# Transposed queries with high and low rows exchanged: by two DMAs instead of by a swapped copy and a second transpose

## The chip, the cores and the metric

The kernel runs on one core of a Trainium2 chip. The metric is the device time of one execution in microseconds (us), the median of several runs. The engines are TensorE (PE in the rows; PEld is its weight load), VectorE (DVE), ScalarE (ACT), GpSimd (POOL) and SyncE (SP, which issues DMAs). A "q" behind an engine's name is its queue of instructions. L619 is line 619 of the kernel.

## The reference, cut to what matters

One layer over a sequence of 1024 frames of width 1024: a mixer of two attention branches, then a SwiGLU feed-forward. The change touches how the queries of both branches reach the score matmuls.

```python
h = rms_norm(x, ln_mix_pre)
z = h @ w_in                      # differential q, k, v | latents | rotary key | gates
q1, q2, k1, k2 = rope(...)        # 8 heads, two 64-wide halves each
o1 = chunk_causal_attention(q1, k1, va, da_scale)
o2 = chunk_causal_attention(q2, k2, va, da_scale)
oa = rms_norm(o1 - lam * o2, da_subln) * (1 - lambda_init)
...
qb_full = concat([qb_nope, rope(qb_rope)])     # 8 heads, 128 + 64 wide
kb_full = concat([kb_nope, rope(k_rope)])      # the rotary key is shared by the heads
ob = chunk_causal_attention(qb_full, kb_full, vb, MLA_QK_DIM ** -0.5)
merged = sigmoid(g_a) * (oa @ w_proj_a) + sigmoid(g_b) * (ob @ w_proj_b)
x = x + rms_norm(merged @ w_o, ln_mix_post)
x = x + rms_norm(swiglu(rms_norm(x, ln_ffn_pre)), ln_ffn_post)
```

All of it is float32. Attention is causal in chunks of 64 frames.

## The kernel before

**High and low parts.** Every float32 operand of a matmul is split into a high part in TensorE's rounded format (float32r) and a low part, the difference. A product is three matmuls: high by high, high by low, low by high (`mm3`, lines 267 to 269). Where the inner dimension is only 64 wide, the kernel puts the high part into rows 0 to 63 and the low part into rows 64 to 127 of one 128-row operand. Keys are held that way: `kT` has the high rows above the low rows. A score tile then takes two matmuls that add up in PSUM (`v` = 0 and 1): one with the query in the same order (high by high plus low by low), one with the query in the exchanged order (low above high). So each query tile is needed transposed in both orders.

**The query tiles before.** A query tile has 128 frames on the partitions, and for each half `m` 64 high columns followed by 64 low columns. `swapped` (lines 615 to 621) has GpSimd copy it with the two column blocks exchanged, two instructions (lines 619 and 620). `pre(i)` then transposes the tile and the swapped copy on TensorE: in differential attention (DA) four transposes into one PSUM bank (lines 689 and 690, twice each, for two halves), in latent attention (MLA) two (lines 904 and 905). ScalarE copies the bank to SBUF, 512 columns (line 693) or 256 (line 908). The result is `Q_[i]`, from which `front(i)` takes `lhsT` by `m` and `v` (lines 707 and 925).

**Stages.** Normalisation, transposed input and the first head's projection come first (to about 66 us). DA runs over eight heads, each over eight query tiles from the last to the first. Beside each head stand fillers: gate tiles, latent projections and the next head's projections. MLA runs over eight heads in the same way, with the next head's projections as fillers; beside its last head stands the first branch projection. After it come the branch and output projections and the feed-forward.

**Order of the work.** The source emits per step x of a head (`pipeline`):

```python
if x + PRE < NT:
    pre(order[x + PRE])      # PRE = 1
if x < NT:
    front(order[x])          # scores, maximum, exponential
...
    back(order[x - depth])   # normalise, transpose the probabilities; depth 1 (DA), 2 (MLA)
```

`tail` (the product with the values) follows every second `back`. This is the order of priority; the order in which each engine gets its instructions is made when the program is built, by a scheduler with its own estimate of durations, and it moves fillers between them. Each engine then works in its own order and waits on semaphores.

**Buffers.** SBUF and PSUM are managed by hand: a zone gives out the block that has been free longest. `z_c` (2048 columns) holds the transposed queries, the swapped copies and a few small tiles; `ps_a` are two PSUM banks that all transposes and the value products share. All DMAs are issued on SP's queue.

Of the kernel before, what the change touches and what calls it, by code (L numbers as in the profile page):

```python
# [12 lines left out]
F32R = mybir.dt.float32r  # L13
# [5 lines left out]
P = 128  # L19
# [150 lines left out]
def kernel(  # L170
# [27 lines left out]
    nc = tc.nc  # L198
# [31 lines left out]
    idr = big.tile([P, P], F32R, name="idr")  # L230
# [9 lines left out]
    def st(tag, n=1):  # L240
        return small.tile([P, n], F32, tag=tag, name=tag)
# [8 lines left out]
    def f32v(ap):  # L250
        return ap.bitcast(F32)
# [48 lines left out]
    z_c, z_ct = Zone(mr, (32768, 34816)), Zone(mr, (34816, AR_COLS))  # L300
# [11 lines left out]
    ps_s, ps_p, ps_a = Banks(mp, 0, 4), Banks(mp, 4, 6), Banks(mp, 6, 8)  # L312
# [299 lines left out]
                       c4[:, 0:nk, 0, half], c4[:, 0:nk, 1, half])  # L612
            tb.free()

    def swapped(q, m):

        b = z_c.alloc(m * P)
        b3 = b.v("p (m c) -> p m c", m=m)
        nc.gpsimd.tensor_copy(b3[:, :, 0:64], f32v(q[:, :, 64:128]))  # L619
        nc.gpsimd.tensor_copy(b3[:, :, 64:128], f32v(q[:, :, 0:64]))  # L620
        return b

    def new_ct(j):
        n = 2 * j + 2
        ct = [z_ct.alloc(512 * min(4, n - g)) for g in range(0, n, 4)]
        last = ct[-1].v("p (k h s) -> p k h s", h=2, s=256)
        nc.gpsimd.memset(f32v(last[:, (n - 1) % 4, :, 0:P]), 0.0)  # L627
        return ct

    def pv(o, ct, vget, j):  # L630
        n = 2 * j + 2
        for kb in range(n):
            c4 = ct[kb // 4].v("p (k h s) -> p k h s", h=2, s=256)
            vh, vl = vget(kb)
            mm3(o, vh, vl, c4[:, kb % 4, 0, :], c4[:, kb % 4, 1, :], kb == 0, kb == n - 1)
# [44 lines left out]
    def da_attn(n, slots, neg_lam, sub8):  # L680
        Q_, P_, CT = {}, {}, {}

        def pre(i):
            q = slots[i // 2]["q"][:, i & 1]
            qx = swapped(q, 2)
            tb = ps_a.alloc()
            for m in range(2):
                a, b = tb.ap[:, m * 256:m * 256 + P], tb.ap[:, m * 256 + P:m * 256 + 256]
                nc.tensor.transpose(a.bitcast(F32R), q[:, m, :], idr)
                nc.tensor.transpose(b.bitcast(F32R), qx.ap[:, m * P:(m + 1) * P], idr)  # L690
            qx.free()
            Q_[i] = z_c.alloc(512)
            nc.scalar.copy(Q_[i].ap, tb.ap)
            tb.free()

        def front(i):
            j = i // 2
            W = P * (i + 1)
            nb = 2 if W > 512 else 1
            qs = Q_.pop(i)  # L700
            nm, ss = st("nm", 2), st("sm", 2)
            pp = []
            for m in range(2):
                sb = ps_s.alloc(nb)
                for p in range(j + 1):
                    for v in range(2):
                        nc.tensor.matmul(sb.ap[:, p * 256:(p + 1) * 256], lhsT=qs.ap[:, m * 256 + v * P:m * 256 + v * P + P],  # L707
                                         rhs=slots[p]["kT"][:, m, :], start=(v == 0), stop=(v == 1))
                pb = f_gen.alloc(W)
                softmax_part(sb.ap, i, m, nm, ss, pb.ap)  # L710
                sb.free()
                pp.append(pb)
            qs.free()
            P_[i] = (pp, ss)

        def back(i):
            pp, ss = P_.pop(i)
            j = i // 2
            if i & 1:
                CT[j] = new_ct(j)  # L720
            rs = st("rs", 2)
            nc.vector.reciprocal(rs, ss)
            bb = st("bb")
            nc.vector.tensor_tensor(out=bb, in0=rs[:, 1:2], in1=neg_lam, op=ALU.mult)
            nc.vector.tensor_scalar_mul(pp[1].ap, pp[1].ap, bb)
            nc.vector.scalar_tensor_tensor(out=pp[0].ap, in0=pp[0].ap, scalar=rs[:, 0:1], in1=pp[1].ap, op0=ALU.mult, op1=ALU.add)
            pp[1].free()
            transposed_probs(pp[0].ap, i, CT[j])
            pp[0].free()

        def tail(j):
            ct = CT.pop(j)
            pb = ps_a.alloc()
            o = pb.ap[:, 0:256]
            pv(o, ct, lambda kb: (slots[kb // 2]["V"][:, kb % 2, 0, :], slots[kb // 2]["V"][:, kb % 2, 1, :]), j)
            for b in ct:
                b.free()
            slots[j]["blk"].free()
            o2, os = f_gen.alloc(256), f_gen.alloc(256)
            nc.scalar.activation(out=o2.ap, in_=o, func=ACTF.Square)  # L740
            nc.scalar.mul(os.ap, o, sub8)  # L741
            pb.free()
            nc.sync.dma_start(s_oa[n * P:(n + 1) * P, j * 256:(j + 1) * 256], os.ap)
            os.free()
            sq = z_c.alloc(512)
            split_sbuf(o2.ap, sq.ap[:, 0:256], sq.ap[:, 256:512], "dve")
            o2.free()

            def sums():
                rb = ps_a.alloc()  # L750
                for h in range(2):
                    nc.tensor.matmul(rb.ap[0:1, 0:256], lhsT=ones_r[:, 0:1], rhs=sq.ap[:, h * 256:(h + 1) * 256],
                                     start=(h == 0), stop=(h == 1))
                sq.free()
                row = f_gen.alloc(256)
                nc.scalar.copy(row.ap[0:1], rb.ap[0:1, 0:256])
                rb.free()
                nc.sync.dma_start(s_ms[n:n + 1, j * 256:(j + 1) * 256], row.ap[0:1])
                row.free()

            return [sums]

        return pipeline(pre, front, back, tail, DA_DEPTH)


# [130 lines left out]
    def mla_attn(M, n, H):  # L896
        vv = H["v"].v("p (t h n d) -> p t h n d", t=NT, h=2, n=2)
        Q_, P_, CT = {}, {}, {}

        def pre(i):  # L900
            q = H["qr"][:, i, :]
            qx = swapped(q.unsqueeze(1), 1)
            tb = ps_a.alloc()
            nc.tensor.transpose(tb.ap[:, 0:P].bitcast(F32R), q, idr)
            nc.tensor.transpose(tb.ap[:, P:2 * P].bitcast(F32R), qx.ap, idr)
            qx.free()
            Q_[i] = z_c.alloc(256)
            nc.scalar.copy(Q_[i].ap, tb.ap[:, 0:256])
            tb.free()

        def front(i):
            j = i // 2
            W = P * (i + 1)
            nb = 2 if W > 512 else 1
            qs = Q_.pop(i)
            nm, ss = st("nm", 2), st("sm", 2)
            sb = ps_s.alloc(nb)
            sl = slice(i * P, (i + 1) * P)
            step = max(W // nb, 256)
            for c in range(nb):  # L920
                ks = slice(c * step, (c + 1) * step)
                o = sb.ap[:, c * 512:c * 512 + step]
                mm3(o, H["q"][:, 0, sl], H["q"][:, 1, sl], H["k"][:, 0, ks], H["k"][:, 1, ks], True, False)
                for v in range(2):
                    nc.tensor.matmul(o, lhsT=qs.ap[:, v * P:(v + 1) * P], rhs=M.kr.ap[:, ks], start=False, stop=(v == 1))
            qs.free()
            pb = f_gen.alloc(W)
            softmax_part(sb.ap, i, 0, nm, ss, pb.ap, W // nb)
            sb.free()
            P_[i] = (pb, ss)  # L930

        def back(i):
            pb, ss = P_.pop(i)
            j = i // 2
            if i & 1:
                CT[j] = new_ct(j)
            rs = st("rs", 2)
            nc.vector.reciprocal(rs[:, 0:1], ss[:, 0:1])
            nc.vector.tensor_scalar_mul(pb.ap, pb.ap, rs[:, 0:1])
            transposed_probs(pb.ap, i, CT[j])  # L940
            pb.free()

        def tail(j):
            ct = CT.pop(j)
            pb = ps_a.alloc()
            o = pb.ap[:, 0:256]
            pv(o, ct, lambda kb: (vv[:, kb, 0, n % 2, :], vv[:, kb, 1, n % 2, :]), j)
            for b in ct:
                b.free()
            os = f_gen.alloc(256)  # L950
            nc.scalar.copy(os.ap, o)
            pb.free()
            nc.sync.dma_start(s_ob[n * P:(n + 1) * P, j * 256:(j + 1) * 256], os.ap)
            os.free()
            if j == 0:
                for b in H["blks"]:
                    b.free()
                if n == NH - 1:
                    M.kr.free()
            return []  # L960

        return pipeline(pre, front, back, tail, MLA_DEPTH)


# [473 lines left out]
```

## Time and profile before

| | |
|---|---|
| median of 3 runs | 2032.49 us (2032.35 to 2034.26) |
| profiled execution | 2036.9 us, span 2035.0 us |
| TensorE busy | 1976.3 us, 97% of the span |
| VectorE, ScalarE, GpSimd busy | 1156.2, 864.2, 541.0 us |
| mean granted clock of TensorE | 0.992 |

The span runs from the first to the last instruction of the profiled execution, which has its own time beside the runs' median. Busy time is the union of an engine's instructions; matmuls are pipelined, and their durations overlap. Issuing a DMA and waiting on a semaphore don't count as busy.

### The profile page before, as it was taken

The page shows a single profiled execution, that of the slowest core. Times are in us where ns is not written, and L with a number is a line of the kernel's source. Part 1 is how long each engine was busy: PE and PEld are TensorE (multiplying, and loading weights), DVE is VectorE, ACT ScalarE, POOL GpSimd, SP SyncE. Part 2 cuts the span into 40 slices and gives each one's busy share as a digit, 9 for nine tenths or more (in the row PEclk, how much of TensorE's full clock was granted, in tenths as well). Part 3 has the DMA queues.
Part 4 walks back from the last instruction along what each step waited for, and adds up shares of the span by engine and source line. Part 5 has one row for each costly group of instructions (what it writes and reads, how often), then busy time and mean ns, then how long its engine had stood idle before and what let it go on. Part 6 is the DMA issues. An engine that isn't in the chain of part 4 may idle for free. (4 is left out here: it accounts for less than half of the span.)

```text
span 2035.0 us, 29108 instructions
## 1 busy us (share of the span) xinstructions
PE 1976.3 (97%) x10656; PEld 1715.3 (84%) x10656; DVE 1156.2 (57%) x2464; ACT 864.2 (42%) x1912; POOL 541.0 (27%) x652
## 2 busy tenths in 40 slices
PE   6999999999999999999999998979999999999998
PEld 6898999999898988988978786757888888888886
DVE  7756757676675667786752354575344444353335
ACT  5445444554544446666653333343333333341102
POOL 2000010200000012222121222356564564462214
PEclk9999999999999999999999999989999999999999
DMA  5212111211212031450043533223222222272204
GB/s 169 69 47 81 44 55 53 57 49 42 77 29 80 29 116 50 130 177 29 32 136 103 176 125 103 85 71 94 73 94 84 71 95 73 95 237 83 83 32 145
DMA packets 148494, 176.52 MB, mean 87 GB/s; under 512 B 13536, under 2 KB 117376, under 8 KB 148352
## 3 DMA queue, kind: packets, MB, share of 16 engines
q1 hardware_dynamic: 148352, 174.68, 27.3%
q8 instruction: 83, 1.36, 0.3%
q14 instruction: 59, 0.48, 0.1%
HBM read 130.54 MB, written 44.11 MB: 86 GB/s over the span
## 5 line engine op out<-in xcount | busy, mean ns | idle before, releaser
L267 PE MATMUL PS<-AR 128*128 128x512 f32 (+3 forms) x2216 | 795.1, 361 | 4.0 <-ACT AR L254 2.5
L269 PE MATMUL PS<-AR 128*128 128x512 f32 (+3 forms) x2216 | 786.3, 356 | 2.6 <-POOL AR L256 2.6
L268 PE MATMUL PS<-AR 128*128 128x512 f32 (+3 forms) x2216 | 784.5, 355 | 3.7 <-POOL AR L256 3.7
L254 ACT CAST AR<-AFm 128x512 fp32r<-128x512 f32 (+4 forms) x514 | 301.7, 610 | 514.1 <-PE PS L1216 207.4
L267 PEld LDWEIGHTS PS<-AR 128*128 128x128 f32 x2216 | 418.1, 189 | 56.8 <-ACT AR L260 3.5
L268 PEld LDWEIGHTS PS<-AR 128*128 128x128 f32 x2216 | 419.0, 189 | 47.8 <-POOL AR L256 4.5
L269 PEld LDWEIGHTS PS<-AR 128*128 128x128 f32 x2216 | 417.9, 189 | 46.3 <-POOL AR L256 3.5
L256 POOL TENSOR_TENSOR AR<-AFm,AR 128x512 fp32r<-128x512 f32 (+4 forms) x203 | 309.2, 1529 | 461.7 <-ACT AR L254 397.4
L1216 PE MATMUL PS<-AR 128*128 128x512 f32 x1848 | 425.7, 392 | 6.1 <-POOL AR L256 4.9
L1216 PEld LDWEIGHTS PS<-AR 128*128 128x128 f32 x1848 | 349.3, 189 | 82.2 <-POOL AR L256 6.2
L256 DVE TENSOR_TENSOR AR<-AFm,AR 128x512 fp32r<-128x512 f32 (+5 forms) x311 | 213.1, 714 | 109.3 <-ACT AR L254 81.8
L260 ACT CAST AR<-PS 128x512 fp32r<-128x512 f32 (+3 forms) x320 | 134.5, 440 | 149.5 <-DVE AFm L388 75.4
L1225 DVE TENSOR_TENSOR AFm<-AFm,PS 128x512 f32<-128x512 f32 x110 | 75.2, 684 | 180.3 <-PE PS L1216 179.6
L261 DVE TENSOR_TENSOR AR<-PS,AR 128x512 fp32r<-128x512 f32 (+3 forms) x320 | 152.9, 496 | 38.0 <-ACT AR L260 36.5
L619 POOL CAST AR<-AR 128x128 fp32r<-128x128 f32 (+1 forms) x128 | 43.1, 337 | 456.0 <-PE PS L690 262.4
L649 ACT ACTIVATE AFm<-PS,nm 128x1024 f32<-128x1024 f32 (+3 forms) x192 | 142.5, 745 | 45.9 <-DVE nm L648 28.8
L648 DVE TENSOR_REDUCE nm<-PS 128x1 f32<-128x1024 f32 (+3 forms) x192 | 143.5, 751 | 3.2
L1288 DVE TENSOR_TENSOR AFm<-AFm,PS 128x512 f32<-128x512 f32 x80 | 54.4, 685 | 103.1 <-PE PS L269 103.1
L1180 DVE TENSOR_TENSOR AFm<-AFm 128x512 f32<-128x512 f32 x66 | 70.4, 1066 | 68.4 <-DMA s_aa<-AFm 29.7
L627 POOL MEMSET AR<- 128x256 f32 x64 | 22.3, 349 | 295.3 <-PE PS L269 200.3
L707 PE MATMUL PS<-AR 128*128 128x256 f32 x640 | 94.9, 290 | 0.1
L609 PE MATMUL PS<-idf,AFm 128*128 128x128 f32 x576 | 88.6, 275 | 2.2 <-ACT AFm L741 0.9
(133 smaller groups left out, 1551.9 us busy)
## 6 DMA issues: line engine op xcount, KB each, us to landing
AFm<-in_w_in_dram SPq DMA_DIRECT2D x72, 192.0 KB
AFm<-in_w_ffn_gate_dram SPq DMA_DIRECT2D x22, 512.0 KB
AFm<-in_w_ffn_up_dram SPq DMA_DIRECT2D x22, 512.0 KB
s_aa<-AFm SPq DMA_DIRECT2D x44, 256.0 KB
AFm<-in_w_ffn_down_dram SPq DMA_DIRECT2D x22, 512.0 KB
AFm<-s_aa SPq DMA_DIRECT2D x22, 512.0 KB
AFm<-in_x_dram SPq DMA_DIRECT2D x16, 512.0 KB
AFm<-in_w_in_dram SPq DMA_DIRECT2D x32, 256.0 KB
```

The lines of the kernel that those rows point to most:

```text
L254: nc.scalar.copy(h, src)
L256: e.tensor_tensor(out=l, in0=src, in1=f32v(h), op=ALU.subtract)
L260: nc.scalar.copy(h, src)
L261: nc.vector.tensor_tensor(out=l, in0=src, in1=f32v(h), op=ALU.subtract)
L267: nc.tensor.matmul(o, lhsT=sh, rhs=mh, start=first, stop=False)
L268: nc.tensor.matmul(o, lhsT=sh, rhs=ml, start=False, stop=False)
L269: nc.tensor.matmul(o, lhsT=sl, rhs=mh, start=False, stop=last)
L609: nc.tensor.transpose(tb.ap[:, q * P:(q + 1) * P], C[:, (g + q) * P:(g + q + 1) * P], idf)
L648: nc.vector.tensor_reduce(out=nm[:, m:m + 1], in_=src, axis=ax, op=ALU.max, negate=True)
L649: nc.scalar.activation(out=dst, in_=src, func=ACTF.Exp, bias=nm[:, m:m + 1], scale=1.0, accum_out=ss[:, m:m + 1])
L707: nc.tensor.matmul(sb.ap[:, p * 256:(p + 1) * 256], lhsT=qs.ap[:, m * 256 + v * P:m * 256 + v * P + P], rhs=slots[p]["kT"][:, m, :], start ...
L1216: nc.tensor.matmul(o, lhsT=v[:, ws, k], rhs=m, start=first and k == 0 and x == 0, stop=k == 3 and x == 2, skip_group_check=True)
```

## The change

`both_orders` takes the place of `swapped`. TensorE transposes each tile once (`m` transposes in place of two times `m`). ScalarE copies the bank, half as many columns as before, into the first half of a block of `z_c`. Two DMAs, issued on ScalarE's queue, then fill the second half: rows 64 to 127 go to partitions 0 to 63 and rows 0 to 63 to partitions 64 to 127. In DA each moves 64 rows of 1 KB, in MLA 64 rows of 512 bytes. In `front` of DA the columns of `lhsT` are now ordered by `v` first, then by `m`.

```diff
-    def swapped(q, m):
-
-        b = z_c.alloc(m * P)
-        b3 = b.v("p (m c) -> p m c", m=m)
-        nc.gpsimd.tensor_copy(b3[:, :, 0:64], f32v(q[:, :, 64:128]))
-        nc.gpsimd.tensor_copy(b3[:, :, 64:128], f32v(q[:, :, 0:64]))
+    def both_orders(q, m):
+
+        tb = ps_a.alloc()
+        for x in range(m):
+            nc.tensor.transpose(tb.ap[:, x * P:(x + 1) * P].bitcast(F32R), q[:, x, :], idr)
+        b = z_c.alloc(2 * m * P)
+        n = m * P
+        nc.scalar.copy(b.ap[:, 0:n], tb.ap[:, 0:n])
+        tb.free()
+        a = f32v(b.ap)
+        nc.scalar.dma_start(a[0:64, n:2 * n], a[64:128, 0:n])
+        nc.scalar.dma_start(a[64:128, n:2 * n], a[0:64, 0:n])
         return b
...
         def pre(i):
-            q = slots[i // 2]["q"][:, i & 1]
-            qx = swapped(q, 2)
-            tb = ps_a.alloc()
-            for m in range(2):
-                a, b = tb.ap[:, m * 256:m * 256 + P], tb.ap[:, m * 256 + P:m * 256 + 256]
-                nc.tensor.transpose(a.bitcast(F32R), q[:, m, :], idr)
-                nc.tensor.transpose(b.bitcast(F32R), qx.ap[:, m * P:(m + 1) * P], idr)
-            qx.free()
-            Q_[i] = z_c.alloc(512)
-            nc.scalar.copy(Q_[i].ap, tb.ap)
-            tb.free()
+            Q_[i] = both_orders(slots[i // 2]["q"][:, i & 1], 2)
...
-                        nc.tensor.matmul(sb.ap[:, p * 256:(p + 1) * 256], lhsT=qs.ap[:, m * 256 + v * P:m * 256 + v * P + P],
+                        nc.tensor.matmul(sb.ap[:, p * 256:(p + 1) * 256], lhsT=qs.ap[:, v * 256 + m * P:v * 256 + m * P + P],
...
         def pre(i):
-            q = H["qr"][:, i, :]
-            qx = swapped(q.unsqueeze(1), 1)
-            tb = ps_a.alloc()
-            nc.tensor.transpose(tb.ap[:, 0:P].bitcast(F32R), q, idr)
-            nc.tensor.transpose(tb.ap[:, P:2 * P].bitcast(F32R), qx.ap, idr)
-            qx.free()
-            Q_[i] = z_c.alloc(256)
-            nc.scalar.copy(Q_[i].ap, tb.ap[:, 0:256])
-            tb.free()
+            Q_[i] = both_orders(H["qr"][:, i, :].unsqueeze(1), 1)
```

## Rows read from the trace of the kernel before

**Rows 1.** Page, part 1: busy time, share and instructions of each engine.

```profile
PE 1976.3 (97%) x10656; PEld 1715.3 (84%) x10656; DVE 1156.2 (57%) x2464; ACT 864.2 (42%) x1912; POOL 541.0 (27%) x652
```

**Rows 2.** Windows, DA stage and MLA stage; the first line names the columns.

```profile
core 0: us, PE busy (x) PEld busy (x) DVE busy (x) ACT busy (x) POOL busy (x), PEclk, DMA share, GB/s
66.00:790.00 724.00, 719.67 (x4513) 659.91 (x4512) 480.73 (x1317) 351.16 (x920) 72.79 (x194) 1.00 0.21 61
790.00:1085.00 295.00, 291.08 (x1842) 256.27 (x1841) 196.93 (x438) 187.03 (x429) 66.55 (x173) 0.99 0.30 96
```

**Rows 3.** Lines on TensorE, 50 to 1090 us: busy us, mean ns, idle before.

```profile
L690 PE MATMUL PS<-idr,AR 128*128 128x128 f32 x128 | 25.5, 244 | 0.0
...
L905 PE MATMUL PS<-idr,AR 128*128 128x128 f32 x64 | 14.9, 233 | 0.0
```

**Rows 4.** Timeline of TensorE in DA: start, us, engine, line, operation.

```profile
66.58 0.29 PE L592 MATMUL PS<-idr,AR 128*128 128x128 f32 x2
...
67.01 0.40 PE L267 MATMUL PS<-AR 128*128 128x512 f32 x1
...
67.48 0.22 PE L689 MATMUL PS<-idr,AR 128*128 128x128 f32 x1
...
67.68 0.25 PE L690 MATMUL PS<-idr,AR 128*128 128x128 f32 x1
...
68.07 0.40 PE L267 MATMUL PS<-AR 128*128 128x512 f32 x1
```

**Rows 5.** Timeline of TensorE in MLA, two stretches.

```profile
808.38 0.22 PE L904 MATMUL PS<-idr,AR 128*128 128x128 f32 x1
...
808.50 0.46 PE L267 MATMUL PS<-AR 128*128 128x512 f32 x1
808.80 0.39 PE L268 MATMUL PS<-AR 128*128 128x512 f32 x1
...
825.15 0.27 PE L609 MATMUL PS<-idf,AFm 128*128 128x128 f32 x1
...
825.50 0.40 PE L267 MATMUL PS<-AR 128*128 128x512 f32 x1
```

**Rows 6.** Lines by shape on ScalarE, 66 to 1085 us.

```profile
L693 ACT CAST AR<-PS 128x512 fp32r<-128x512 f32 x64 | 36.9, 587 | 78.8 <-PE PS L690 78.6
...
L908 ACT CAST AR<-PS 128x256 fp32r<-128x256 f32 x64 | 23.9, 373 | 21.7 <-PE PS L905 19.7 <-DVE PS L642 1.8
...
L260 ACT CAST AR<-PS 128x128 fp32r<-128x128 f32 x88 | 23.5, 267 | 77.5 <-DVE AFm L388 72.4 <-PE PS L609 3.1 <-DVE bb L724 1.1
```

**Rows 7.** Timeline, two small DMAs on SP and a waiter on GpSimd.

```profile
391.24 0.34 SPq L527 DMA_DIRECT2D s_kr<-AR  x1
...
393.87 0.44 POOL L619 CAST AR<-AR 128x128 fp32r<-128x128 f32 x1 [1.85 <-DMA s_kr<-AR]
...
822.52 0.50 SPq L972 DMA_DIRECT2D AFm<-s_ms  x1
```

**Rows 8.** Timeline, eviction and scores of the first and the last short tile.

```profile
68.10 0.58 ACT L693 CAST AR<-PS 128x512 fp32r<-128x512 f32 x1
...
68.77 0.46 PE L707 MATMUL PS<-AR 128*128 128x256 f32 x2
...
1036.95 0.37 ACT L908 CAST AR<-PS 128x256 fp32r<-128x256 f32 x1 [0.98 <-PE PS L905]
...
1038.76 0.70 PE L925 MATMUL PS<-AR 128*128 128x448 f32 x1
```

**Rows 9.** Windows: two whole MLA heads, and two short stretches.

```profile
965.00:1002.00 37.00, 36.98 (x251) 33.83 (x252) 24.14 (x58) 25.67 (x58) 5.32 (x21) 1.00 0.09 30
1002.00:1036.00 34.00, 30.77 (x191) 25.89 (x191) 27.72 (x55) 24.51 (x52) 7.11 (x21) 0.98 0.48 155
1036.00:1040.00 4.00, 4.00 (x13) 3.10 (x12) 1.14 (x2) 1.69 (x3) 3.45 (x7) 0.50 0.30 92
862.00:865.00 3.00, 3.00 (x19) 2.38 (x18) 0.83 (x2) 1.40 (x4) 1.50 (x7) 1.00 1.03 308
```

## The prediction, on record before the changed kernel ran

> **What bounds the kernel now.** I read the busy times first. TensorE is busy for 97% of the span (its own weight loads, which overlap, for 84%), no other engine for more than 57% [rows 1]. Then the stretches in which the changed lines run. Differential attention (DA, eight heads) fills 66 to 790 us, latent attention (MLA, eight heads) 790 to 1085 us, and in both TensorE is busy for 99% of the time (719.67 of 724, 291.08 of 295) [rows 2]. The reader is to see that here the length of the stage is the sum of TensorE's steps. ScalarE stands at 49% and 63%, GpSimd at 10% and 23%: what is taken from them shortens nothing by itself, and what is given to them must first make TensorE wait. Last I read the timeline from step to step, since the busy time of a matmul includes its latency and can't be added.
>
> **The change part by part.**
>
> *Transposes removed.* Before, each query tile has four transposes in DA and two in MLA; after, two and one. That takes away 128 (line 690) and 64 (line 905) of the counts in [rows 3]. Their mean of 233 to 244 ns is not their price, since they overlap. From the timeline: four transposes and the 512-column matmul behind them take 68.07 - 67.48 = 0.59 us; two and such a matmul 67.01 - 66.58 = 0.43 us [rows 4]. Two fewer save 0.16 us, 64 times: 10.2 us. In MLA two and a 512-column matmul take 808.80 - 808.38 = 0.42 us, one and such a matmul 825.50 - 825.15 = 0.35 us [rows 5]. One fewer saves 0.07 us, 64 times: 4.5 us. Together 14.7 us, all of it on the engine that sets the stage.
>
> The Trainium skill (TensorE: Matmul & The Clock Gate, Part 4: PE-mode transpose) gives about 275 ns for a 128x128 transpose in a kernel. By that the 192 would be worth 52.8 us (an estimate from that page). The trace agrees with it for the duration of one, 233 to 244 ns, and not for what one costs in a row of them.
>
> *GpSimd's swapped copies removed.* 256 short casts leave an engine that is 10% and 23% busy. TensorE's first wait of this kind would be at the second pair of transposes, and the timeline shows the four starting within 0.20 us, from 67.48 to 67.68 [rows 4]. Worth nothing; the cover is that GpSimd is early. If it had been late somewhere, that would be a small gain more.
>
> *The eviction on ScalarE becomes shorter.* 128x512 took 587 ns and 128x256 takes 373, so 0.21 us less in DA; in MLA 128x256 becomes 128x128, 373 to 267 ns, 0.11 us less [rows 6].
>
> *Two DMA issues added on ScalarE's queue per query tile*, 256 in all. No DMA is issued there before, so I bound by SP's: 0.34 us for a 64 KB store of 128 rows, 0.50 us for a transfer of 64 rows [rows 7]. ScalarE's instructions behind them stand still for 0.7 to 1.0 us per tile. Its load becomes 351 - 14 + 44 to 64, so 381 to 401 of 724 us in DA (53 to 55%), and 187 - 7 + 44 to 64, so 224 to 244 of 295 us in MLA (76 to 83%). In DA that is room enough. In MLA the evictions of the score and projection tiles queue behind these issues, and TensorE waits for the banks they free. I price this together with the next point, since the same spare matmuls cover both.
>
> *A wait added: the exchanged rows.* The second matmul of each score tile (value 1 of v) now needs both transfers. The nearest row is the 64 KB store from the same zone: issued at 391.24, its buffer's next writer released at 393.87, so 2.63 us [rows 7]. The second transfer is issued 0.34 us after the end of the eviction, so the operand is there 2.97 us after it, and with the shorter eviction 2.75 us (DA) and 2.85 us (MLA) later than the whole operand is before. A transfer may be quicker than that row (the far end is no loss at all), or slower: between 862 and 865 us, at the start of an MLA head, the 16 DMA engines are fully busy (share 1.03) [rows 9].
>
> Where does this meet a matmul? Mostly nowhere: each tile's transposes stand one stage ahead of its scores. I compared, for all 128 tiles, the end of the eviction with the start of the second score matmul. In 15 of 64 DA tiles and 29 of 64 MLA tiles this is less than 2.75 and 2.85 us; the first and the last of these 44 are in [rows 8] (in the first the scores start 0.09 us after the eviction's end at 68.68). They are the first tile of each head, the last tile of most, and in MLA further ones in between. What is missing adds up to 31.3 us in DA and 50.6 us in MLA.
>
> These 81.9 us are lost only where nothing else can be put in front. The order on TensorE isn't the source's: the trace shows projection and gate matmuls (lines 267 to 269) between the transposes and the scores, and this order is made anew for the changed program. In DA each head has gate, latent and next-head projections to draw on, so I take a twentieth as uncovered: 1.6 us. In MLA the only filler is the next head's projections. Seven of its eight heads leave at most 0.5 us of TensorE idle, as the row for 965 to 1002 us does; the eighth, 1002 to 1036, leaves 3.2 us [rows 9]. I take one part in eight as uncovered: 6.3 us.
>
> *Sum:* -14.7 + 1.6 + 6.3 = -6.8 us. The profiled execution took 2036.9 us (span 2035.0), so 2030.1; the median of the runs is 4.4 us lower, 2032.5, so 2025.7 us.
>
> **The rivals.**
>
> *Slower: in MLA the exchanged rows come late.* Speaking for it: half-covered heads, DMA engines fully busy at a head's start, ScalarE at up to 83%. There is also an amplifier. After 3.2 us of idle near 1034 us the granted clock stood at 0.50 from 1036 to 1040 us, the 1.2 GHz level [rows 9], so a hole of some length is paid for again in slow matmuls. Half of the 50.6 us uncovered gives 25.3 + 1.6 - 14.7 = +12 us, 2044 to 2045 us. It decides as soon as more than (14.7 - 1.6) / 50.6, some 26% of the MLA shortage, stays open. Against it: TensorE had almost no hole in either stage, with longer chains than this (scores, maximum, exponential, transposes) to cover.
>
> A second way into the slower case: the two halves run one after the other. If the second sets out only when the first has landed, the operand comes 2.3 us later (2.63 - 0.34), 73 tiles are short by 74.1 + 143.8 us, and with my two shares the cost is 3.7 + 18.0 us: +7 us, 2039.5 us. It has 6 of the 32 hundredths below. The Trainium skill (DMA: Bandwidth & Descriptors, Rules for kernel authors) says that two transfers to disjoint partition halves serialize, and advises one over 128 partitions. No row here shows such a pair.
>
> *No difference:* the 14.7 us are given back, because the waits on ScalarE and on the transfers take about as much (11 to 19 us uncovered), or because the new order of the instructions is by chance a few us worse elsewhere. 2028.5 to 2036.5 us.
>
> *More gain:* the waits are all covered and the transposes cost more than their steps say. Full cover alone gives 2017.8 us. If a transpose cost its whole duration, 128 x 244 and 64 x 233 ns would be 46.1 us [rows 3], and 1986 us with full cover; to that I give 2 in 100.
>
> **How the numbers follow.** A difference of 0.2% (4.1 us) is about what a measurement of this kernel tells from no change; the three runs before lie within 0.1%. My forecast (up to an eighth of the shortage uncovered) has 0.46, and the larger gain 0.02: faster 0.48. No difference 0.20. Slower 0.32, of which 0.26 for late rows in MLA and 0.06 for halves that run one after the other. The likeliest case alone reaches from 2018 (all covered) to 2028.4. Since both signs have weight, the range goes from 2016 to 2046 us.
>
> **What would show it.** Right: 128 transposes in DA and 64 in MLA; TensorE's busy share in 66 to 775 us still 99%; the DA stage some 8 us shorter; the MLA stage shorter or longer by few us; waits of the score matmuls (lines 707 and 925 of before) for a DMA of a few us in all. Wrong: such waits adding up to more than 13 us, or the granted clock below 1.00 at MLA head starts (late rows); ScalarE's issues lasting well over 0.5 us or its evictions released late with TensorE waiting for them (ScalarE as the bound); second halves landing 2 us or more behind the first. The prediction is wrong too if the stages shrink by far more than 14.7 us, or if the time goes in a stretch that the change doesn't touch, which would be the new order and not the transposes.

## The result and the profile after

The changed kernel is slower. Its median is 2048.61 us (2043.56 to 2049.42) against 2033.38 us (2032.35 to 2034.68) for the kernel before, a ratio of 1.0070 (95% interval 1.0058 to 1.0082). The forecast was 2025.7 us with a range of 2016 to 2046 us. In the profiled executions the span goes from 2035.0 to 2046.2 us; that is 11.2 us and not 15.2, because the profiled execution before was itself 3.5 us above its median and the one after 0.6 us below.

The first row of the page, part 1, looks harmless: TensorE has 192 instructions fewer and is busy 5.4 us less than in [rows 1], and GpSimd loses 256 casts.

```profile
PE 1970.9 (96%) x10464; PEld 1698.9 (83%) x10464; DVE 1158.9 (57%) x2464; ACT 844.2 (41%) x1912; POOL 468.9 (23%) x396
```

The windows of the two stages, which answer to [rows 2], show where to look (columns as there). DA has kept its 99% on TensorE and is some 11 us shorter. MLA is longer, and TensorE is idle in it for 22.3 us where it was idle for 3.9.

```profile
66.00:775.00 709.00, 704.74 (x4353) 643.52 (x4351) 478.86 (x1304) 335.59 (x911) 35.20 (x65) 1.00 0.26 74
785.00:1094.00 309.00, 286.73 (x1729) 244.56 (x1728) 194.38 (x428) 173.12 (x413) 33.05 (x50) 0.98 0.32 101
```

From here on a stage is measured by its score matmuls. The first one of MLA starts at 796.1 us before and at 784.7 after: DA gained 11.4 us. From the first to the last one MLA takes 285.3 us before and 309.4 after: MLA lost 24.1. What comes behind gained 1.5.

The lines by shape answer to [rows 3] and [rows 6]: 192 transposes in place of 384 (L619, both stages), and the evictions at 374 and 270 ns, 0.21 and 0.10 us shorter as forecast (L622).

```profile
L619 PE MATMUL PS<-idr,AR 128*128 128x128 f32 x192 | 35.1, 238 | 0.5 <-DVE AR L261 0.5
...
L622 ACT CAST AR<-PS 128x256 fp32r<-128x256 f32 x64 | 23.8, 374 | 65.3 <-PE PS L619 52.4 <-DMA AR<-AR 11.1 <-PE PS L269 1.5
...
L622 ACT CAST AR<-PS 128x128 fp32r<-128x128 f32 x64 | 16.5, 270 | 35.2 <-DMA AR<-AR 16.2 <-PE PS L619 16.1 <-PE PS L913 2.6
```

The waits of the weight load in MLA (us in total, times, longest) name two suspects. The score matmuls wait for the exchange (L913 for a DMA), as forecast. But the first matmul of a product (L267) waits longer, for the exponential on ScalarE (L655) to give a score bank back, and for other evictions.

```profile
PEld PS L267 <- ACT AFm L655: 10.2, 18, 1.6
PEld PS L913 <- DMA AR<-AR: 7.1, 7, 2.1
PEld PS L267 <- DVE AR L261: 5.3, 6, 1.4
PEld PS L267 <- DVE AR L264: 4.1, 3, 2.0
```

The timeline of ScalarE at the start of an MLA head shows what it is late with (ACTq is its queue issuing a DMA; columns start, us, engine, line, operation, and the idle time before it).

```profile
820.17 0.26 ACT L622 CAST AR<-PS 128x128 fp32r<-128x128 f32 x1
820.33 0.59 ACT L263 ACTIVATE AR<-PS 128x512 fp32r<-128x512 f32 x1
820.46 0.47 ACTq L625 DMA_DIRECT2D AR<-AR  x1
820.97 0.61 ACTq L626 DMA_DIRECT2D AR<-AR  x1
821.62 0.43 ACT L622 CAST AR<-PS 128x128 fp32r<-128x128 f32 x2 [0.69 <-PE PS L619]
821.91 0.47 ACTq L625 DMA_DIRECT2D AR<-AR  x1
822.42 0.61 ACTq L626 DMA_DIRECT2D AR<-AR  x1
823.12 0.55 ACTq L625 DMA_DIRECT2D AR<-AR  x1
823.72 0.61 ACTq L626 DMA_DIRECT2D AR<-AR  x1
824.37 0.27 ACT L622 CAST AR<-PS 128x128 fp32r<-128x128 f32 x1 [2.31 <-DMA AR<-AR]
824.53 0.60 ACT L263 ACTIVATE AR<-PS 128x512 fp32r<-128x512 f32 x1
```

Two tiles' exchanges stand back to back from 821.91 to 824.33. The next eviction starts only then, and behind it the eviction of a projection tile (L263). The profile puts the 2.31 us of idle down to a DMA; what fills them, but for 0.2 us, is four issues (0.47 + 0.61 + 0.55 + 0.61 = 2.24 us, of which the first 0.14 lie beside the eviction before). From 820.17 to 824.37 us ScalarE did 1.2 us of work.

Some of the holes are paid for twice. Windows in the seventh MLA head:

```profile
1033.00:1035.00 2.00, 0.00 (x0) 0.00 (x0) 2.00 (x4) 1.30 (x5) 0.00 (x0) 1.00 0.36 59
1035.00:1037.00 2.00, 1.92 (x7) 1.73 (x8) 1.88 (x6) 1.28 (x2) 0.00 (x0) 0.58 0.84 303
1037.00:1039.00 2.00, 2.00 (x11) 1.73 (x11) 1.31 (x3) 1.21 (x2) 0.00 (x0) 0.57 0.90 285
...
1043.00:1045.00 2.00, 0.50 (x2) 0.30 (x2) 0.45 (x2) 1.10 (x2) 0.00 (x0) 1.00 0.72 210
...
1047.00:1049.00 2.00, 2.00 (x10) 1.96 (x10) 1.12 (x1) 0.83 (x1) 2.00 (x2) 0.51 0.85 246
```

Behind 2 us without a matmul the granted clock is 0.58 and 0.57 for the next four, and behind the nearly empty stretch from 1043 to 1045 it falls to 0.51 (0.50 is the 1.2 GHz level). Before, there was one such stretch near the end of this head, [rows 9]. This second payment is small. In the windows of the eight heads the granted clock was below 1.00 in two, before and after:

```profile
1003.00:1037.00 34.00, 30.77 (x191) 25.95 (x190) 27.09 (x54) 23.74 (x51) 7.57 (x19) 0.97 0.49 159
1037.00:1081.00 44.00, 43.98 (x235) 37.77 (x235) 19.13 (x41) 23.07 (x41) 9.57 (x12) 0.95 0.25 73
```

```profile
859.00:898.00 39.00, 35.90 (x204) 29.70 (x203) 26.30 (x54) 18.56 (x50) 3.00 (x6) 0.96 0.59 195
...
1007.00:1052.00 45.00, 36.07 (x197) 29.59 (x196) 30.00 (x56) 26.50 (x55) 6.36 (x7) 0.92 0.46 143
```

Length times what is missing of the clock gives 3.2 us before and 5.2 us after, so some 2 of the 24.1 us (an estimate from these rows); the idle time grew by 18.4.

### The profile page after: what moved, and what is told of

The parts are those of the page before. It is cut to its first block, busy times and chain, and to the rows that moved or that the text cites. A ratio compares the mean times of both kernels' runs of the same rounds, so it can differ in the third digit from the quotient of the medians.

```text
span 2046.2 us, 28684 instructions
## 1 busy us (share of the span) xinstructions
PE 1970.9 (96%) x10464; PEld 1698.9 (83%) x10464; DVE 1158.9 (57%) x2464; ACT 844.2 (41%) x1912; POOL 468.9 (23%) x396
## 5 line engine op out<-in xcount | busy, mean ns | idle before, releaser
L267 PE MATMUL PS<-AR 128*128 128x512 f32 (+3 forms) x2216 | 797.0, 362 | 14.0 <-ACT AFm L655 3.8
L254 ACT CAST AR<-AFm 128x512 fp32r<-128x512 f32 (+4 forms) x514 | 301.5, 610 | 508.5 <-PE PS L1204 207.0
L267 PEld LDWEIGHTS PS<-AR 128*128 128x128 f32 x2216 | 419.4, 190 | 70.6 <-ACT AFm L655 10.2
L268 PEld LDWEIGHTS PS<-AR 128*128 128x128 f32 x2216 | 419.9, 190 | 47.1 <-POOL AR L256 4.5
L269 PEld LDWEIGHTS PS<-AR 128*128 128x128 f32 x2216 | 419.3, 190 | 45.8 <-POOL AR L256 3.3
L1204 PEld LDWEIGHTS PS<-AR 128*128 128x128 f32 x1848 | 348.7, 189 | 80.2 <-POOL AR L256 4.8
L655 ACT ACTIVATE AFm<-PS,nm 128x1024 f32<-128x1024 f32 (+3 forms) x192 | 142.1, 743 | 77.9 <-DVE nm L654 56.8
L703 PEld LDWEIGHTS PS<-AR 128*128 128x128 f32 x640 | 83.6, 189 | 6.9 <-ACT AFm L655 3.0
```

The lines of the kernel that those rows point to most:

```text
L254: nc.scalar.copy(h, src)
L267: nc.tensor.matmul(o, lhsT=sh, rhs=mh, start=first, stop=False)
L268: nc.tensor.matmul(o, lhsT=sh, rhs=ml, start=False, stop=False)
L269: nc.tensor.matmul(o, lhsT=sl, rhs=mh, start=False, stop=last)
L655: nc.scalar.activation(out=dst, in_=src, func=ACTF.Exp, bias=nm[:, m:m + 1], scale=1.0, accum_out=ss[:, m:m + 1])
L1204: nc.tensor.matmul(o, lhsT=v[:, ws, k], rhs=m, start=first and k == 0 and x == 0, stop=k == 3 and x == 2, skip_group_check=True)
```

## The experiments

Two theories. **A, ScalarE's queue:** the two issues take 1.08 us per tile in the order of ScalarE's instructions, and evictions and exponentials behind them come late. **B, late rows:** the exchange makes the second order arrive later than a second transpose did, and the scores, and all behind them, wait.

All kernels, in the order in which they are told. "MLA begins" and "MLA stage" are starts of score matmuls in each profile (before: 796.1 and 285.3 us).

| kernel | median us | ratio to before, 95% | MLA begins | MLA stage |
|---|---|---|---|---|
| the change | 2048.61 | 1.0070 [1.0058, 1.0082] | 784.7 | 309.4 |
| e1, DA only | 2024.68 | 0.9958 [0.9945, 0.9970] | 785.2 | 285.9 |
| e2, MLA only | 2065.02 | 1.0156 [1.0142, 1.0170] | 796.1 | 313.5 |
| e3, no exchange | 2019.73 | 0.9933 [0.9918, 0.9948] | 782.4 | 284.9 |
| e4, unread DMAs, ScalarE | 2049.72 | 1.0076 [1.0063, 1.0090] | 796.7 | 297.3 |
| e12, unread DMAs, SP | 2035.91 | 1.0012 [1.0003, 1.0021] | 795.3 | 286.5 |
| e5, exchange on GpSimd | 2048.76 | 1.0074 [1.0059, 1.0089] | 785.5 | 305.8 |
| e6, exchange on SP | 2034.66 | 1.0007 [0.9998, 1.0016] | 783.8 | 298.3 |
| e7, ScalarE, two tiles ahead | 2053.89 | 1.0100 [1.0084, 1.0117] | 785.5 | 314.3 |
| e10, before, two tiles ahead | 2041.03 | 1.0037 [1.0023, 1.0052] | 796.9 | 292.3 |
| e8, GpSimd, two tiles ahead | 2036.03 | 1.0015 [1.0006, 1.0024] | 787.7 | 295.6 |
| e9, SP, two tiles ahead | 2028.13 | 0.9977 [0.9967, 0.9987] | 783.1 | 289.8 |
| e13, SP, only first tiles wait | 2035.02 | 1.0004 [0.9995, 1.0013] | 784.0 | 296.1 |
| e14, SP, all but first tiles wait | 2024.10 | 0.9959 [0.9945, 0.9973] | 783.7 | 288.0 |
| e11, DA only, SP | 2021.87 | 0.9945 [0.9932, 0.9958] | 784.3 | 285.4 |

A stage comes from one profiled execution, and executions of one kernel differ, those of e6 from 2031.5 to 2039.4 us. The profiled one was 4.4 us below its median in e4, 3.8 below in e5, 2.0 below in e9 and 4.7 above in e6. Where the code of MLA is the same, its stage agrees within 0.6 us (before, e1, e11) or differs by 4.1 (the change, e2). So a difference of 2 to 4 us between two stages is not shown to be more than that; where a size matters, the medians stand beside it.

### One part alone: e1 and e2

In e1 MLA's `pre`, in e2 DA's `pre` (and its order of columns) is that of the kernel before, with `swapped`.

> The change in DA alone; MLA keeps the swapped copy and the second transpose. Stage arithmetic (both theories below): the changed kernel's DA stage ended 11 us earlier than before (score matmuls over at 774.9 instead of 785.9 us) and its MLA stage gave 24 us back, so DA alone comes to 2033 - 11 = 2022 us (2019 to 2026). Chance theory (the loss is the new order of instructions and not bound to MLA): anywhere between 2025 and 2045 us.

> The change in MLA alone; DA as before. Stage arithmetic: DA unchanged, MLA 24 us longer, so 2057 us (2052 to 2062). Chance theory: within 5 us of before, 2028 to 2038 us.

The change is a gain in DA and a loss in MLA, and the loss alone is larger than expected: 28.2 us of stage, 4.1 more than the same code loses in the change. A part of this goes with the clock, 0.97 over e2's stage against 0.98 in the change.

### The change without its DMAs: e3

The kernel leaves the exchanged order out: the second matmul of a score tile takes the first order again. The lines of MLA; DA's `front` is changed in the same way.

```diff
-        nc.scalar.dma_start(a[0:64, n:2 * n], a[64:128, 0:n])
-        nc.scalar.dma_start(a[64:128, n:2 * n], a[0:64, 0:n])
...
-                    nc.tensor.matmul(o, lhsT=qs.ap[:, v * P:(v + 1) * P], rhs=M.kr.ap[:, ks], start=False, stop=(v == 1))
+                    nc.tensor.matmul(o, lhsT=qs.ap[:, 0:P], rhs=M.kr.ap[:, ks], start=False, stop=(v == 1))
```

> Single transposes and short evictions in both stages, but no DMAs and no exchanged block: the second matmul of each score tile takes the first order once more (so the low parts are paired wrongly and the output is not the reference's). This is the removal alone. By the steps of the prediction: 14.7 us less than before, 2018.7 us (2016 to 2022), DA stage about 10 us and MLA stage about 4.5 us shorter. If the transposes cost more than their steps, the stages shrink further; if the MLA loss comes from having fewer transposes or from the new order, MLA is still longer than before here.

The total came as expected, its division did not. DA gained 13.7 us (796.1 - 782.4) and MLA 0.4 us. The windows of MLA, before and in e3 (one row of each kernel):

```profile
796.00:1081.00 285.00, 281.08 (x1790) 248.53 (x1789) 193.44 (x428) 180.28 (x412) 64.31 (x170) 0.99 0.29 94
```

```profile
782.00:1067.00 285.00, 278.01 (x1732) 241.81 (x1731) 194.76 (x429) 174.38 (x414) 34.02 (x50) 0.99 0.29 95
```

TensorE has 3.1 us less to do in the same 285 us: what the transposes gave back became idle time. In this pair, MLA was not limited by TensorE's steps, in spite of its 99%. It is one pair: a lead of two tiles, with the same instructions in a new order, moved the stage by 7.0 us (e10 below), so that a transpose in MLA is worth nothing is not shown.

### DMAs that nobody reads: e4 and e12

The kernel before, with two transfers of the size of MLA's exchange after each eviction, into a block that no instruction reads; on ScalarE's queue (e4) or on SP's (e12, `nc.sync`).

```diff
             tb.free()
+            a = f32v(Q_[i].ap)
+            u = z_c.alloc(P)
+            nc.scalar.dma_start(f32v(u.ap)[0:64], a[64:128, 0:P])
+            nc.scalar.dma_start(f32v(u.ap)[64:128], a[0:64, 0:P])
+            u.free()
```

> The kernel before, with two added DMAs per MLA query tile on ScalarE's queue (32 KB each, as in the changed kernel) into a block that nothing reads; copies and transposes as before. Theory A (ScalarE's queue: two issues of 0.47 and 0.61 us and the wait for the eviction hold up evictions and exponentials): the MLA stage becomes longer by 10 to 25 us, 2043 to 2058 us. Theory B (the score matmuls wait for the rows to land, about 2 us after the issue): nothing reads them, so no change, 2031 to 2036 us.

> The kernel before, with two DMAs per MLA query tile whose rows nobody reads, now on SP's queue; on ScalarE's the same transfers cost 11.9 us of MLA stage and 16 us of time. ScalarE's queue is what costs: MLA stage 283 to 288 us, total 2031 to 2036 us. The traffic of the transfers itself, or the order that the scheduler makes for a program with them, costs: MLA stage some 297 us, total 2045 to 2050 us.

Here nothing waits for a row, and half of the loss is there: 12.0 us of MLA stage with ScalarE's queue, 1.2 us with SP's. So it is neither the traffic nor the issues as such, but the engine in whose order they stand: 10.8 us, or 13.8 by the medians (2049.72 against 2035.91). (e12's whole time is still 2.9 us over before, of which 1.2 is this stage.) The same wait is the longest of e4 and an ordinary one in e12 (waits of the weight load in MLA, e4 and then e12):

```profile
PEld PS L267 <- ACT AFm L649: 11.7, 18, 2.6
```

```profile
PEld PS L267 <- ACT AFm L649: 3.5, 9, 1.2
```

### The exchange on other queues: e5 and e6

`nc.scalar.dma_start` becomes `nc.gpsimd.dma_start` (e5) or `nc.sync.dma_start` (e6).

> The changed kernel with all 256 DMAs issued on GpSimd's queue, which is busy for 11% of the MLA stage after the change. The unread DMAs on ScalarE's queue made the MLA stage 12 us longer, the changed kernel's MLA stage is 24 us longer than before. If the two parts add up (ScalarE's queue 12 us, late rows 12 us), the first goes away: 2048.6 - 12 = 2036 us (2032 to 2041), with the MLA stage 10 to 14 us longer than before. If late rows are all of it (theory B), no less than 2046 us, more if the path by GpSimd is slower. If ScalarE's queue is all of it (theory A), 2022 to 2026 us.

> The changed kernel with all 256 DMAs issued on SP's queue, between the loads and stores, where in the trace of before issues wait up to 22 us for a buffer. If the parts add up and SP's queue were free: 2036 us. Since a small transfer now stands behind a load or store that waits, the rows come later than on ScalarE's queue for some tiles, in DA too: 2040 to 2080 us. Theory A without B would make even that harmless: 2022 to 2028 us.

With SP's queue the stage is 298.3 us, 11.1 less than with ScalarE's; that agrees with the 10.8 of the unread transfers (by the medians the whole kernel is 14.0 us shorter, against 13.8). What is left, 13.0 us over before, is not ScalarE's queue. In it the first matmul of a product waits for the exponential as long as in the change, since late scores make a late exponential too (e13 below shows one); so this wait by itself doesn't tell the two theories apart (e6):

```profile
PEld PS L267 <- ACT AFm L655: 10.7, 13, 2.3
```

GpSimd's queue gained 3.6 us of stage in its profile and nothing in the median. By its expectation that spoke for late rows alone; SP's queue shows that it was GpSimd's queue that made them late. It issues 0.52 us each, the rows wait there in turn, and the score matmuls wait 14.0 us for them, against 7.3 in the change. The lines of the two DMAs in MLA, in e5 (durations min/median/max, and from issue to landing):

```profile
L625 POOL DMA_DIRECT2D AR<-AR x64: 516/523/536, 788.4 to 1083.3; - x64
...
DMA to landing us min/median/max: 1.7/1.7/5.5
L626 POOL DMA_DIRECT2D AR<-AR x64: 516/523/626, 788.9 to 1083.8; - x64
...
DMA to landing us min/median/max: 1.7/1.7/5.6
```

The second half sets out 0.52 us after the first and lands as soon after its own issue: it doesn't wait until the first has landed. Each half's own packets take 0.30 us in this trace, and those of the second begin 0.2 us after the first's have ended (medians over MLA), so the two rarely moved data at the same time.

### The rows a tile earlier: e7 and e10, e8 and e9

`pipeline` gets a lead of two tiles in MLA: e7 is the change, e10 the kernel before as control; e8 and e9 are e5 and e6.

```diff
-        for x in range(PRE):
+        for x in range(ahead):
             pre(order[x])
...
-            if x + PRE < NT:
-                pre(order[x + PRE])
+            if x + ahead < NT:
+                pre(order[x + ahead])
```

> The changed kernel with the transposes of MLA standing two query tiles ahead of the scores in place of one; DMAs on ScalarE's queue. Theory B (late rows): each tile's rows have some 4 us more to land, the waits for DMAs at the score matmuls of MLA (7 us now) mostly vanish and the MLA stage is 10 to 24 us shorter: 2025 to 2038 us. Theory A (ScalarE's queue): the same issues stand in front of the same evictions, and at a head's start one more of them stands before the first exponential: 2045 to 2053 us.

> Control: the kernel before with the transposes of MLA two query tiles ahead. Nothing waits for them now, so no change by either theory: 2030 to 2036 us. If it is faster or slower by more than that, the order and the shared PSUM banks have a part in the run with two ahead, and that run is read against this one.

> The changed kernel with its DMAs issued on GpSimd's queue (no issue on ScalarE's), and MLA's transposes two tiles ahead of the scores instead of one, so that the rows have a tile more of time to arrive. Its control is the kernel before with two tiles ahead (MLA stage 292.3 us, total 2041.0). Late rows that hold score tiles open: waits of the score matmuls for a DMA all but gone, MLA stage 290 to 296 us, total 2028 to 2034 us. GpSimd's own queue is late (0.52 us per issue, and the casts that feed it wait behind): the MLA stage stays near the 306 us that GpSimd's queue gave with one tile ahead, total 2042 to 2048 us.

> The same with the DMAs on SP's queue. With one tile ahead that had an MLA stage of 298.3 us. Late rows as the remainder: the stage falls to that of the control (292.3 us, two tiles ahead, no DMAs), so 290 to 294 us and a total of 2027 to 2031 us (control's 2041.0 less the 12 us that DA gains). If the remainder is something else (contention of transfers, loads and stores that stand behind the exchanges in SP's queue, the new order): the stage is 298 us or more, total 2034 to 2045 us. On ScalarE's queue two tiles ahead gave 314.3 us; whatever SP's queue gives below that is the price of ScalarE's queue at equal lead.

On ScalarE's queue the lead takes the waits for the rows away (score matmuls wait 1.4 us for a DMA in place of 7.3) and gives no time: 314.3 us, 22.0 over its control. So with ScalarE's queue the rows' lateness is not what ends last. On SP's queue the same lead brings 289.8 us, 2.5 below the control. At equal lead the two queues are 24.5 us apart, more than twice the 11.1 at one tile's lead, and most of it shows as TensorE waiting for late exponentials (e7, then e9):

```profile
PE PS L267 <- ACT AFm L655: 20.7, 9, 4.6
```

```profile
PE PS L267 <- ACT AFm L655: 4.7, 5, 1.8
```

The control missed its expectation of no change: it is itself 7.0 us worse than before, with the same instructions in a new order. That the exchange is a small gain in MLA at this lead is not shown, since 2.5 us is within what profiled executions differ by. On GpSimd's queue (e8) the lead takes 10.2 us off and leaves 3.3 over the control; the stage came as expected, the time 2 us above.

### Which tiles wait: e13 and e14

e6 with one edit, which leaves the exchanged order out of some tiles. In e13 only the first tile of each head takes the exchanged rows, in e14 (`i < NT - 1`) all others do.

```diff
-                    nc.tensor.matmul(o, lhsT=qs.ap[:, v * P:(v + 1) * P], rhs=M.kr.ap[:, ks], start=False, stop=(v == 1))
+                    nc.tensor.matmul(o, lhsT=qs.ap[:, v * P:(v + 1) * P] if i == NT - 1 else qs.ap[:, 0:P], rhs=M.kr.ap[:, ks], start=False, stop=(v == 1))
```

> The changed kernel with its DMAs on SP's queue (2034.7 us, MLA stage 298.3 us, 13 us over the kernel before), except that in MLA only the first query tile of each head takes the exchanged rows; the other seven tiles' second matmul takes the first order again, so that they don't wait for the transfers, which all still run (their output is therefore not the reference's). The transposes of a head's first tile have no tile of the same head to run beside. If the first tiles are where the rows are late: the MLA stage stays at 294 to 299 us. If the tiles in the middle and at the end of the heads are: 284 to 288 us, total about 2022 to 2025 us. If it is spread: about 288 to 294 us.

> The complement: every tile but the first of each MLA head takes the exchanged rows, and the first takes the first order again (its output is therefore not the reference's); all transfers run, on SP's queue. If the first tiles are where the rows are late: MLA stage 284 to 289 us, total 2022 to 2025 us. If the later tiles are: 294 to 299 us, total 2031 to 2035 us. If both kernels come out near 298 us, or both near 286 us, the loss is not a sum of single late tiles but sits in the order made for the whole program.

Eight tiles cost 10.8 us, the other 56 cost 2.7; together that is about the 13.0 of e6. Timelines of the seventh head, before and in e13, show how. Before, all four rotary matmuls of the first tile (L925) follow the eviction at once, and its exponential (L649) starts 2.67 us behind the first of them, from 1002.60 to 1005.27.

```profile
1002.60 1.19 PE L925 MATMUL PS<-AR 128*128 128x512 f32 x4
...
1005.27 1.12 ACT L649 ACTIVATE AFm<-PS,nm 128x1024 f32<-128x1024 f32 x1
```

```profile
998.97 0.73 PE L913 MATMUL PS<-AR 128*128 128x512 f32 x2
...
999.18 0.47 SPq L625 DMA_DIRECT2D AR<-AR  x1
...
999.70 0.59 SPq L626 DMA_DIRECT2D AR<-AR  x1
...
1002.42 0.61 PE L913 MATMUL PS<-AR 128*128 128x512 f32 x2
...
1005.61 1.11 ACT L655 ACTIVATE AFm<-PS,nm 128x1024 f32<-128x1024 f32 x1
```

In e13 the two matmuls of the second order stand 3.45 us behind those of the first, with the next tile's scores and projection matmuls between them, and the exponential (L655) 6.64 us behind. TensorE doesn't wait for the DMA here; the order made for this program has put other work in front. But that work is used up earlier, and behind it TensorE has holes: over the eight heads, the 8 us from the first rotary matmul on hold this much work (sum rows of the windows, 64 us each: before, e13, e14).

```profile
sum 64.00, PE 64.00 PEld 56.39 DVE 50.43 ACT 42.71 POOL 15.35; mean PE 8.00 PEld 7.05 DVE 6.30 ACT 5.34 POOL 1.92
```

```profile
sum 64.00, PE 57.58 PEld 46.18 DVE 34.54 ACT 33.05 POOL 5.59; mean PE 7.20 PEld 5.77 DVE 4.32 ACT 4.13 POOL 0.70
```

```profile
sum 64.00, PE 63.87 PEld 54.38 DVE 44.69 ACT 35.43 POOL 1.85; mean PE 7.98 PEld 6.80 DVE 5.59 ACT 4.43 POOL 0.23
```

TensorE had no hole there before, 6.4 us in e13, 0.1 us in e14. The other 4 us of e13's loss lie outside these windows. The order that was made has its part in the lateness: on ScalarE, too, a cast of 1.05 us (L254, from 1004.65) stands right before the exponential of e13 above. Whether another order, with the same transfers, would lose less was not tested.

### A version that beats both: e11

e1 with its DMAs on SP's queue: the change in DA alone.

> The change in DA alone, its DMAs on SP's queue; MLA as in the kernel before. DA's stage gained 10.9 us with the issues on ScalarE's queue and 12.3 us with SP's, and MLA without the change stood at 286 us. Both theories give 2021 us (2019 to 2024), a us or two below the DA-only kernel with ScalarE's queue (2024.7). If SP's queue delays the loads and stores of other stages: 2025 us or more.

2021.87 us, a ratio of 0.9945 (0.9932 to 0.9958) to the kernel before: the fastest of those that leave nothing out.

## Why the prediction was wrong, step by step

**What bounds the kernel: right for DA, not borne out in MLA.** The reading "busy for 99%, so the length is the sum of TensorE's steps" held in DA, where steps taken away shortened the stage, and failed in MLA as far as e3 shows, which took 64 transposes away for 0.4 us. [rows 9] already showed a head with 3.2 us of idle.

**Transposes: mis-sized both ways.** Forecast 10.2 us in DA and 4.5 in MLA, measured 13.7 and 0.4 (e3; 2.5 at two tiles' lead, e9 against e10, with what is left of the waits in it). The 0.4 and the 2.5 are within what single profiles differ by. In DA that is 0.21 us per tile in place of 0.16; e3 takes the casts and part of the eviction away too, so their share in it can't be told apart.

**Waits in DA: right.** 1.6 us forecast; 1.9 measured (13.7 less the 11.8 of e11), or 1.4 (e6, which gains 12.3), and ScalarE's queue adds 0.9 (e1 against e11; the medians have 2.8).

**Two issues on ScalarE's queue: the step that failed.** Their length was forecast at 0.7 to 1.0 us per tile and is 1.08. The failure is the sentence "I price this together with the next point, since the same spare matmuls cover both". So the issues got no price of their own. They are a second cost, and with one tile of lead the two add: 11 us of MLA for the queue alone (11.1 by the change against e6, 10.8 by e4 against e12; some 14 by the medians), with ScalarE only 56% busy in the stage (173.12 of 309 us; issues are not in it). The forecast had it at 76 to 83% with issues, and took what was left for room. But here the queue was late long before it was full. Nor is its price a constant: at two tiles of lead it is 24.5 us. Of the prediction's own signs of being wrong, the one for ScalarE came, evictions released late with TensorE waiting; the one for late rows, waits of more than 13 us, didn't (7.3 us).

**Uncovered waits in MLA: right kind, half the size.** One part in eight of 50.6 us was 6.3; measured 13.4, one part in four (e6 against e3). The prediction had named the tiles, "the first tile of each head", and those carry 10.8 (e13). Counted in its way they are short by 18.6 of the 50.6 us, so more than half of that stayed uncovered, and of the other 32.0 less than a tenth (2.7, e14). It averaged the two kinds.

**The rivals.** "In MLA the exchanged rows come late" gave 2044 to 2045 us and had the sign and the stage. Its mechanism is half of the loss, so that its number is so near is luck; its amplifier was there (clock 0.58 and 0.51 above), but worth some 2 us. "The halves run one after the other" is refuted by e5's landings. The Trainium skill (DMA: Bandwidth & Descriptors, Rules for kernel authors) says that two transfers to disjoint partition halves serialize. For these 32 KB halves, issued 0.52 us apart, the trace shows no wait of one for the other, 1.7 us each from its own issue; whether they would slow each other if they moved data at once, no run here shows. "Full cover" would have needed 2017.8 us; e3, which has no waits at all, is at 2019.73.

**The sum.** In stages, from before to e3, e6 and the change: -13.7 + 1.4 + 0.9 = -11.4 in DA, -0.4 + 13.4 + 11.1 = 24.1 in MLA, so +12.7; the rest of the program gives 1.5 back, and the profile has +11.2. The forecast had -6.8. The medians differ by 15.2 us, so the range ended 2.6 us too low.

**Left open.** With two tiles of lead on SP's queue the first exponential of the seventh head is about as late as in e13 (6.43 us behind the first rotary matmul against 6.64), and TensorE is idle for 4.0 of the 64 us at the head starts, yet the stage loses only 4.5 us to before. Why the lateness costs less there was not settled; a change of lead also changes the order of all the instructions, as the control shows (7.0 us).

## What to carry to other kernels

A DMA belongs on the queue of an engine that nothing waits for: its issue takes its place in that engine's order, and here the queue alone decided between 2048.6 and 2034.7 us. That the engine has little to do is not enough: on GpSimd's queue the rows came later, and the time was 2048.8. Price a longer way to an operand at the places where nothing stands in front of it, the first tile of each loop, and not by a share of all tiles. Before counting a saved step as saved time, leave it out in the stage and see whether the stage shrinks: a busy share of 99% of overlapping matmuls was the limit in one stage and, as far as one pair of runs shows, not in the other.

## What the runs showed of the hardware

A transfer of 64 rows between partitions holds the issuing queue for about as long whichever engine issues it: medians in MLA, in the change (ScalarE) and in e6 (SP).

```profile
L625 ACTq DMA_DIRECT2D AR<-AR x64: 468/468/694, 785.0 to 1085.2; - x64
...
L626 ACTq DMA_DIRECT2D AR<-AR x64: 468/609/1673, 785.5 to 1085.7; - x64
```

```profile
L625 SPq DMA_DIRECT2D AR<-AR x63: 461/467/1017, 785.2 to 1073.4; - x63
...
L626 SPq DMA_DIRECT2D AR<-AR x63: 581/588/1502, 785.7 to 1073.9; - x63
```

GpSimd's 0.52 us (e5) is close too. What differed was what stands behind the issue. The Trainium skill (DMA: Bandwidth & Descriptors, Issuing engines are not separate DMA queues) says that starting DMAs on several engines at once saves only the sequencer's time to initiate them, usually small beside the DMA itself. Here that time is not small, 0.47 and 0.61 us on ScalarE beside 1.7 us to land (e5), and taking it from ScalarE's queue was worth 14 us (2048.61 against 2034.66).
